# A hybrid decoder layer on one core: two branches' accumulators are copied out of PSUM by ScalarE, and VectorE multiplies the copies in a queue of lower priority

## The chip, the cores and the metric

The kernel runs on one core of a Trainium2 chip. The core has five engines that run side by side, each through a fixed list of instructions of its own: TensorE (PE in the rows; its weight loads stand apart as PEld), VectorE (DVE), ScalarE (ACT), GpSimd (POOL) and SyncE (SP), which issues the transfers here. An engine stops at an instruction whose operands are not ready, and everything behind it in its list waits too. Weights and activations lie in SBUF; PE writes its sums into PSUM, a small memory of banks. The metric is the device time of one execution, in microseconds (us).

## The reference, cut to what matters

One decoder layer is applied to 1024 prompt tokens and 32 sample tokens (8 sequences of 4), with a width of 1024. From a normalised input `h` four branches are computed: A a diagonal state space model (SSM), B a gated convolution, C a gated delta rule, D stick-breaking attention. Each gives 256 values a token. They are projected to the full width, each is multiplied by a sigmoid gate, and the four are added:

```
branches = jnp.stack([y_a, y_b, y_c, y_d], axis=2)
br    = jnp.einsum('blnw,nwd->blnd', branches, p['w_branch'])
gates = jax.nn.sigmoid(h @ p['w_gate']).reshape(bsz, L, N_BRANCH, D_MODEL)
mixed = jnp.sum(gates * br, axis=2) @ p['w_o']
x = layer_norm(ALPHA_DN * x + (1.0 + g1) * mixed, p['ln1_g'], p['ln1_b'])
```

Behind it come the feed-forward part and a second norm. The change is in the product `gates * br` of two of the four branches.

## The kernel before, in words

**Tiling.** The 1056 tokens are three blocks of 352 (`TB`), the width is eight slabs of 128 channels (`m`). A value is kept as the sum of two half-precision parts, so a product takes three matmuls (`mm3`, line 87 in the rows). One gate tile, 128 channels by 352 tokens, is a sum of 24 matmuls `gps<-h,whl` into one PSUM bank. The projection of the branch to the same channels is six matmuls `gps<-y,wbr` into a second bank, `pb`. Both come from one pool of three banks, `gps`; the conditioning product (`ada_slab`, matmuls `gps<-chl,whl`) takes its banks there too.

**The gate step** (`gates`, lines 1472 to 1495). ScalarE takes the tanh of the gate sum into an SBUF tile `gth` (line 1490; the sigmoid is half of one plus a tanh). VectorE forms `(gth + 1) * pb` with one scalar_tensor_tensor (STT for short), which reads `pb` in PSUM (line 1494, or line 1492 for the first branch). GpSimd adds the product to the running sum `mix` (`merge`, line 1523). `gates(1)` with `first=True` serves branch B and is not touched. `gates(3)` for D and `gates(2)` for C, eight slabs of three blocks each, are the 48 tiles in question. The gates of A (`gates7`, lines 1755 to 1773) use other code: an STT with a PSUM operand at line 1770 and an addition of two SBUF tiles at line 1519, both of the same 128x352 size.

**Weights.** `load_w` brings a slab of 512 KB into one of three tiles `wraw` (transfers `wraw<-in_w_gate`, `wraw<-in_w_ada`); ScalarE scales it (line 105) and makes the upper half-precision part (line 108), GpSimd the remainder (line 114, `whl<-wraw,whl`). Only then is a `wraw` tile free for the next transfer.

**Order.** The Tile framework fixes each engine's list when the kernel is built. Each instruction carries a priority from the stream in which it was written, a lower number goes first among those that its planner holds to be ready: `hot` -8 million, `sup` -4 million, the ordinary text and `br` from 0, `br2` 2 million, `lo` 4 million, `bg` 8 million. Gate matmuls are `lo`: they fill PE between the chains of branches C and A. The tanh, the STT and the merge are `sup`.

**Stages.** The 48 tiles run beside two chains. First the delta rule (lines 890 to 1145). Then the SSM (`ssm`): parameters and tables of cosine and sine (`cs`, `sn`, `tw`, complex multiplications at line 1220, on VectorE and GpSimd), projected matrices (`car`, `cai`, `ab`, `bd`, transposed by PE to `sps`), a small recurrence that goes through DRAM (`kd`, `tt`, line 1358), the scan (`gg`, `hr`, `hi`), the output `yo`, then GELU and GLU (`gs`, `gx`, `yh`, lines 1440 to 1468). Last come the sums for `gates7` (`r`, `tf`, lines 1710 to 1719 and 116).

Of the kernel before, what the change touches and what calls it, by code (L numbers as in the profile page):

```python
# [9 lines left out]
F32 = mybir.dt.float32  # L10
F16 = mybir.dt.float16
I32 = mybir.dt.int32
AF = mybir.ActivationFunctionType
ALU = mybir.AluOpType
# [3 lines left out]
P = 128  # L18
# [7 lines left out]
TB = 352  # L26
# [47 lines left out]
class Builder:  # L74
# [1397 lines left out]
    def gates(self, n, y, first, last, ms=range(KD), ada=0):  # L1472

        nc, I = self.nc, self.I
        pg = self.pg
        for m in ms:
            for _ in range(ada):
                self.ada_slab(self.ada_next)
                self.ada_next += 1
            if m % 4 == 0:  # L1480
                self.branch_w(n * 2 + m // 4)
            w = self.load_w(I["w_gate"][n * KD + m])
            for b in range(NTB):
                ps = self.gtile()
                xh, xl = self.hx(b * TB, TB)
                self.gemm(ps[:, :TB], w, KD, xh, xl)
                pb = self.branch(y, m, b)
                with self.sup:
                    th = pg.tile([P, TB], F32, name="gth", tag="gth", bufs=3)
                    nc.scalar.activation(th, ps[:, :TB], AF.Tanh, scale=IS / 2)  # L1490
                    if first:
                        nc.vector.scalar_tensor_tensor(self.mix[b][:, m], th, 1.0, pb, op0=ALU.add, op1=ALU.mult)
                    else:
                        nc.vector.scalar_tensor_tensor(th, th, 1.0, pb, op0=ALU.add, op1=ALU.mult)  # L1494
                        self.merge(m, b, th, last)

    def branch_w(self, i):
        nc = self.nc
# [496 lines left out]
def build(ctx, tc, I, O, stop=None):  # L1995
    B = Builder(ctx, tc, I, O)
    B.wraw_bufs, B.whl_bufs = 3, 4
    B.consts()
    B.wp = B.pool("w")
    B.gp = B.gp2 = B.pool("gps", bufs=3, space=PSUM)  # L2000
    hp = B.pool("hp")
    yp = B.pool("yp", bufs=2)
    B.make_h(hp)
    B.prep_consts()
    if stop:
        B.attention(yp)
        if stop == "B":
            B.conv_branch(yp)
        if stop == "C":
            B.delta(yp)  # L2010
            B.delta_sample()
            B.delta_rec(yp)
        if stop == "A":
            B.ssm_u()
            B.ssm(yp)
        return B
    def between():
        B.conv_branch(yp)
        B.ssm_u()
        B.px = B.pool("mx", side="right")  # L2020
        B.mix = [B.px.tile([P, KD, TB], F32, name="mix%d" % b, tag="mx", bufs=NTB) for b in range(NTB)]
        B.pg = B.pool("gate", side="right")
        B.gates(1, B.yB, True, False, range(0, GSPLIT))

    B.attention(yp, between)
    B.delta(yp, lambda i: B.gates(1, B.yB, True, False, range(GSPLIT + i, GSPLIT + i + 1)))
    with B.br2:
        B.delta_sample()
    B.delta_rec(yp)
    B.gates(3, B.yD, False, False, ada=A3)  # L2030
    B.gates(2, B.yC, False, False, range(2 * G7), ada=A2)
    B.ssm(yp)
    g7 = B.pool("gate7", side="right")
    B.np = None
    B.up_t = g7
    B.gp = B.pool("gps7", bufs=5, space=PSUM)
    Tf = g7.tile([P, 4, 2, 4, NTB, HB], F16, name="tf")
    for b in range(NTB):
        for q in (0, 2):
            B.sums7(B.h, Tf, b, g7.tile([P, 8 * HB], F32, name="r7", tag="r7"), slice(q, q + 2))  # L2040
    B.xh7 = B.forms7(B.h, Tf)
    B.sk = B.pool("gate7w", side="right")
    B.ska = B.sk
    B.gates7(2, B.yC, False, range(G7, KD // 2))
    B.gates7(0, B.yA, True, range(KD // 2))
    B.free(B.gp, B.gp2, yp, hp, B.ska, g7, B.pg)
    B.np = B.pool("nps2", space=PSUM)
    B.gp = B.pool("gps2", bufs=6, space=PSUM)
    B.px1 = B.pool("x1", side="right")
    B.ph2 = B.pool("h2", side="right")  # L2050
    B.afp = B.pool("af")
    B.mixer_out()
    B.ffn()
    B.close()
    return B
# [125 lines left out]
```

## Time and profile before

| | |
|---|---|
| median of 3 runs | 1922.05 us (1920.45 to 1927.18) |
| the profiled execution | 1922.55 us, its span 1920.8 us |
| granted TensorE clock, mean of the span | 0.96 |
| busy: PE, DVE, ACT, POOL | 90%, 67%, 51%, 50% |

Times in rows are us from the start of the span. An engine's busy share is an average over the span; how its work is spread is seen by stretches. An entry in square brackets behind an instruction is the time for which its engine sat idle before it, with the instruction that ended the wait.

### The profile page before, as it was taken

The numbers are of one execution on the slowest core, as the hardware profiler recorded it, in microseconds if no ns is written. First come the engines' busy times: TensorE is split into PE (matmuls) and PEld (weight loads), VectorE is DVE, ScalarE is ACT, GpSimd is POOL, SyncE is SP. The second block draws the span as 40 slices with busy tenths as digits, with TensorE's granted clock in tenths as the row PEclk, the third lists the DMA queues.
The fourth block names the chain that finished last, engine by engine and source line by source line (L and its number), as shares of the span: only waits on it lengthen the run. The fifth ranks groups of instructions, "written<-read, shape, count | busy, mean of one in ns | idle before, by whom it ended". The sixth has DMA issues, their size and how long they took to land.

```text
span 1920.8 us, 36538 instructions
## 1 busy us (share of the span) xinstructions
PE 1736.0 (90%) x14985; PEld 1202.0 (63%) x14985; DVE 1289.1 (67%) x2134; ACT 988.2 (51%) x1836; POOL 963.0 (50%) x952
## 2 busy tenths in 40 slices
PE   7899999999899998788689899988998999989996
PEld 3466666666666665555367555556776677767765
DVE  6763677659576756377986479777556656765648
ACT  4643454465655545235564655645575545554434
POOL 1827311222354545744550643278676667766633
PEclk9999999999999999899799999998999999999999
DMA  8222221121311112312331430001111112111112
GB/s 311 76 91 69 67 59 34 39 68 55 90 52 57 56 52 87 73 42 79 107 114 66 145 121 1 1 23 51 49 62 50 47 43 67 56 37 53 50 28 91
DMA packets 63616, 130.60 MB, mean 68 GB/s; under 512 B 16408, under 2 KB 35928, under 8 KB 63192
## 3 DMA queue, kind: packets, MB, share of 16 engines
q1 hardware_dynamic: 61912, 124.07, 20.9%
q0 software_dynamic: 1536, 4.20, 0.7%
q8 instruction: 117, 1.92, 0.4%
q14 instruction: 51, 0.42, 0.1%
HBM read 117.36 MB, written 10.88 MB: 67 GB/s over the span
## 4 chain that ended last, share of the span: by engine, by line
PE 40%; DVE 27%; ACT 10%; POOL 8%; DMA 8%; issue 5%; SPq 1%; ACTq 0%; DVEq 0%; POOLq 0%
PE gps L87 29%; DMA wraw<-in_w_up 2%; DVE ring L116 2%; PE x L87 2%; DVE af L1862 2%; POOL whl L1631 2%; DMA wraw<-in_w_down 1%; PE nps L87 1%; DVE dacc L758 1%; DVE af L1850 1%; PE dp L87 1%; DMA wraw<-in_w_gate 1%; PE z L87 1%; PE pada L87 1%; PE sps L87 1%
## 5 line engine op out<-in xcount | busy, mean ns | idle before, releaser
L87 PEld LDWEIGHTS <-whl 128*128 128x128 f16 x6992 | 629.1, 100 | 383.8 <-issue 91.1
L87 PE MATMUL gps<-h,whl 128*128 128x352 f16 (+1 forms) x4344 | 694.7, 315 | 48.0 <-ACT ct L1682 14.9
L87 PEld LDWEIGHTS <-wf 128*128 128x128 f16 x2232 | 198.9, 100 | 70.4 <-issue 12.0
L1631 POOL TENSOR_TENSOR whl<-wraw,whl 128x512 f16<-128x512 f32 (+1 forms) x136 | 166.3, 1234 | 95.2 <-ACT whl L1630 93.3
L114 POOL TENSOR_TENSOR whl<-wraw,whl 128x1024 f16<-128x1024 f32 (+1 forms) x66 | 150.5, 2281 | 85.4 <-ACT whl L108 83.6
L1679 DVE TENSOR_TENSOR ct<-ct,gps 128x352 f32<-128x352 f32 (+1 forms) x114 | 50.9, 449 | 189.8 <-ACT ct L1682 100.8
L1631 POOL TENSOR_TENSOR wf<-wraw,wf 128x512 f16<-128x512 f32 (+1 forms) x102 | 128.2, 1267 | 97.5 <-ACT wf L1630 95.6
L105 ACT ACTIVATE wraw<-wraw 128x1024 f32<-128x1024 f32 (+2 forms) x96 | 96.4, 1005 | 135.1 <-DMA wraw<-in_w_gate 45.7
L87 PE MATMUL gps<-tf,whl 128*128 128x176 f16 (+1 forms) x1152 | 145.9, 285 | 20.9 <-ACT ct L1682 16.3
L87 PE MATMUL gps<-ring,whl 128*128 128x352 f16 (+1 forms) x864 | 103.8, 276 | 8.1 <-ACT ct L1682 5.2
L87 PE MATMUL gps<-y,wbr 128*128 128x352 f16 x576 | 103.2, 313 | 6.7 <-DVE gth L1494 2.3
L1682 ACT ACTIVATE ct<-gps 128x352 f32<-128x352 f32 (+1 forms) x174 | 65.7, 393 | 77.4 <-PE gps L87 50.5
L1622 ACT ACTIVATE wraw<-wraw 128x1024 f32<-128x1024 f32 (+1 forms) x68 | 66.4, 976 | 75.2 <-DMA wraw<-in_w_down 37.8
L1523 POOL TENSOR_TENSOR mix<-mix,gth 128x352 f32<-128x352 f32 x48 | 53.0, 1104 | 99.1 <-DVE gth L1494 88.3
L87 PE MATMUL gps<-mix,wo 128*128 128x352 f16 x576 | 89.7, 316 | 5.3 <-DVE mix L118 2.4
L116 DVE TENSOR_TENSOR ring<-af,ring 128x352 f16<-128x352 f32 (+2 forms) x134 | 87.5, 684 | 5.6 <-ACT ring L108 5.6
L1630 ACT ACTIVATE whl<-wraw 128x512 f16<-128x512 f32 (+1 forms) x136 | 76.7, 585 | 26.8 <-POOL wraw L1635 13.5
L108 ACT ACTIVATE whl<-wraw 128x1024 f16<-128x1024 f32 (+1 forms) x82 | 84.9, 1035 | 3.6 <-DMA wraw<-in_w_ada 3.1
L87 PE MATMUL gps<-h,wf 128*128 128x352 f16 (+1 forms) x624 | 78.5, 281 | 7.8 <-DVE gth L1494 6.2
L108 ACT ACTIVATE ring<-af 128x352 f16<-128x352 f32 (+2 forms) x134 | 54.5, 430 | 56.0 <-DVE af L1862 46.5
L87 PEld LDWEIGHTS <-wo 128*128 128x128 f16 x576 | 56.4, 99 | 39.1 <-issue 4.2
L87 PEld LDWEIGHTS <-wbr 128*128 128x128 f16 x576 | 55.5, 98 | 36.5 <-issue 7.1
(622 smaller groups left out, 3364.9 us busy)
## 6 DMA issues: line engine op xcount, KB each, us to landing
wraw<-in_w_up SPq DMA_DIRECT2D x44, 512.0 KB, 3.5
wraw<-in_w_gate SPq DMA_DIRECT2D x32, 512.0 KB, 3.5
wraw<-in_w_ada SPq DMA_DIRECT2D x32, 512.0 KB, 3.6
wraw<-in_w_in SPq DMA_DIRECT2D x20, 512.0 KB, 3.7
wraw<-in_w_down SPq DMA_DIRECT2D x24, 384.0 KB, 3.1
x<-in_xT SPq DMA_DIRECT2D x12, 704.0 KB, 8.5
araw<-in_w_ada SPq DMA_DIRECT2D x16, 512.0 KB, 10.2
wraw<-in_w_branch SPq DMA_DIRECT2D x8, 512.0 KB, 3.6
```

What stands on the lines that cost most here:

```text
L87: self.nc.tensor.matmul(out, lhsT=lhsT, rhs=rhs, start=start, stop=stop, skip_group_check=resume)
L105: nc.scalar.activation(src, src, AF.Copy, scale=scale)
L108: nc.scalar.activation(hi, src, AF.Copy, scale=scale)
L114: nc.gpsimd.tensor_tensor(lo, src, hi, op=ALU.subtract)
L116: nc.vector.tensor_tensor(lo, src, hi, op=ALU.subtract)
L1523: nc.gpsimd.tensor_tensor(o, o, g, op=ALU.add)
L1622: nc.scalar.activation(raw, raw, AF.Copy, scale=SW)
L1630: nc.scalar.activation(hi, src, AF.Copy)
L1631: nc.gpsimd.tensor_tensor(lo, src, hi, op=ALU.subtract)
L1679: add = lambda o, p: nc.vector.tensor_tensor(o, o, p, op=ALU.add)
L1682: nc.scalar.activation({0: c11, 2: c12, 3: c22}[f], ps, AF.Copy)
L1862: sub = lambda o, p, q: nc.vector.tensor_tensor(o, p, q, op=ALU.subtract)
```

## The change

For the 48 tiles, ScalarE now does two things: the tanh of the gate sum, as before, and a plain copy of the branch sum `pb` from PSUM into a new SBUF tile `pbc` (four buffers, a pool `gate_b` of its own). VectorE multiplies in place, `(gth + 1) * pbc`, from two SBUF tiles, and this STT and the merge behind it are written in `br2` (2 million) instead of `sup` (-4 million). The number of instructions on PE, DVE, POOL and SP stays; ACT has 48 more.

```
                     if first:
                         nc.vector.scalar_tensor_tensor(self.mix[b][:, m], th, 1.0, pb, op0=ALU.add, op1=ALU.mult)
                     else:
-                        nc.vector.scalar_tensor_tensor(th, th, 1.0, pb, op0=ALU.add, op1=ALU.mult)
-                        self.merge(m, b, th, last)
+
+                        pc = self.pb.tile([P, TB], F32, name="pbc", tag="pbc", bufs=4)
+                        nc.scalar.activation(pc, pb, AF.Copy)
+                if not first:
+                    with self.br2:
+                        nc.vector.scalar_tensor_tensor(pc, th, 1.0, pc, op0=ALU.add, op1=ALU.mult)
+                        self.merge(m, b, pc, last)
...
     B.delta(yp, lambda i: B.gates(1, B.yB, True, False, range(GSPLIT + i, GSPLIT + i + 1)))
+    B.pb = B.pool("gate_b", side="right")
...
-    B.free(B.gp, B.gp2, yp, hp, B.ska, g7, B.pg)
+    B.free(B.gp, B.gp2, yp, hp, B.ska, g7, B.pb, B.pg)
```

In the changed kernel the lines behind the edit stand five or six lines further down: the copy is L1496, the STT L1499, the merge L1528.

Since the framework works the order out anew, other instructions move too. Three places follow.

ScalarE, in the SSM's first part, the list before: tanh (L1490) and scaling (L105) alternate.

```order
L294 ACTIVATE adat<-gps,c_b_ada 128x9
L108 ACTIVATE whl<-wraw 128x1024
L1490 ACTIVATE gth<-gps 128x352
L105 ACTIVATE wraw<-wraw 128x1024
L1490 ACTIVATE gth<-gps 128x352
L105 ACTIVATE wraw<-wraw 128x1024
L1338 ACTIVATE bq<-sps 128x512 x4
```

The same place in the changed kernel:

```order
L294 ACTIVATE adat<-gps,c_b_ada 128x9
L108 ACTIVATE whl<-wraw 128x1024
L1490 ACTIVATE gth<-gps 128x352
L1496 ACTIVATE pbc<-gps 128x352
L105 ACTIVATE wraw<-wraw 128x1024 x2
L1490 ACTIVATE gth<-gps 128x352
L1496 ACTIVATE pbc<-gps 128x352
L1490 ACTIVATE gth<-gps 128x352
L108 ACTIVATE whl<-wraw 128x1024
L1496 ACTIVATE pbc<-gps 128x352
L1338 ACTIVATE bq<-sps 128x512 x4
```

The second tanh now stands behind two scalings instead of one, and three copies stand ahead of `bq`, which belongs to the SSM.

GpSimd, in the same stretch, before: two weight remainders (L114) stand in the chain of cosine and sine tables.

```order
L1220 TENSOR_TENSOR cs<-cs,tw 128x8x8
L1220 TENSOR_TENSOR tw<-sn,cs 128x8x8
L1220 TENSOR_TENSOR cs<-cs 128x8x16
L1220 TENSOR_TENSOR sn<-sn,tw 128x8x8
L1523 TENSOR_TENSOR mix_1940<-mix_1940,gth 128x352
L1220 TENSOR_TENSOR tw<-sn 128x8x16
L1220 TENSOR_TENSOR sn<-cs,sn 128x8x16
L1220 TENSOR_TENSOR cs<-cs,tw 128x8x16
L114 TENSOR_TENSOR whl<-wraw,whl 128x1024
L1220 TENSOR_TENSOR tw<-sn,cs 128x8x16
L1220 TENSOR_TENSOR cs<-cs 128x8x32
L114 TENSOR_TENSOR whl<-wraw,whl 128x1024
```

The same place in the changed kernel:

```order
L1220 TENSOR_TENSOR cs<-cs,tw 128x8x8
L114 TENSOR_TENSOR whl<-wraw,whl 128x1024
L1220 TENSOR_TENSOR tw<-sn,cs 128x8x8
L1220 TENSOR_TENSOR cs<-cs 128x8x16
L114 TENSOR_TENSOR whl<-wraw,whl 128x1024
L1528 TENSOR_TENSOR mix_1941<-mix_1941,pbc 128x352
L1220 TENSOR_TENSOR sn<-sn,tw 128x8x8
L1528 TENSOR_TENSOR mix_1939<-mix_1939,pbc 128x352
L1220 TENSOR_TENSOR tw<-sn 128x8x16
```

Both remainders move forward in the list: seven instructions of the list before that stood ahead of the first now stand behind it, among them six pieces of the tables.

VectorE, at the end of the same stretch, before:

```order
L1220 TENSOR_TENSOR big<-piv,bd 128x8x128
L1220 TENSOR_TENSOR ab<-prv,bd 128x1024
L1494 SCALAR_TENSOR_TENSOR gth<-gth,gps 128x352
L1220 TENSOR_TENSOR ab<-ab,big 128x1024
L1220 TENSOR_TENSOR big<-piv,bd 128x8x128
L1494 SCALAR_TENSOR_TENSOR gth<-gth,gps 128x352
L1220 TENSOR_TENSOR ab<-ab,big 128x1024
```

The same place in the changed kernel:

```order
L1220 TENSOR_TENSOR big<-piv,bd 128x8x128
L1220 TENSOR_TENSOR ab<-prv,bd 128x1024
L1220 TENSOR_TENSOR ab<-ab,big 128x1024
L1499 SCALAR_TENSOR_TENSOR pbc<-gth,pbc 128x352
L1220 TENSOR_TENSOR big<-piv,bd 128x8x128
L1220 TENSOR_TENSOR ab<-ab,big 128x1024
```

One STT still stands ahead of the last `ab`, now with the last `big` behind it as well.

## Rows read from the trace of the kernel before

**Rows 1.** The page: busy time of each engine, and the chain that ended last.
```profile
PE 1736.0 (90%) x14985; PEld 1202.0 (63%) x14985; DVE 1289.1 (67%) x2134; ACT 988.2 (51%) x1836; POOL 963.0 (50%) x952
...
PE 40%; DVE 27%; ACT 10%; POOL 8%; DMA 8%; issue 5%; SPq 1%; ACTq 0%; DVEq 0%; POOLq 0%
```

**Rows 2.** Busy us by stretch: PE, PEld, DVE, ACT, POOL; then PE's granted clock.
```profile
546.00:735.00 189.00, 178.64 (x2324) 119.50 (x2323) 121.33 (x260) 99.51 (x182) 95.48 (x82) 0.98 0.17 55
735.00:876.00 141.00, 113.61 (x798) 76.03 (x798) 80.23 (x181) 49.27 (x113) 76.50 (x76) 0.89 0.29 75
876.00:985.00 109.00, 80.03 (x624) 52.45 (x623) 103.57 (x122) 67.50 (x111) 58.98 (x42) 0.84 0.30 99
```

**Rows 3.** Busy us in the scan, columns as in rows 2.
```profile
818.00:855.00 37.00, 28.01 (x219) 18.36 (x219) 35.33 (x46) 13.60 (x30) 20.64 (x11) 0.95 0.15 48
```

**Rows 4.** Line 1494, the multiplication: durations (ns) and what it waited for.
```profile
L1494 DVE SCALAR_TENSOR_TENSOR gth<-gth,gps x48: 494/513/522, 549.8 to 941.7; 128x352 f32<-128x352 f32 x48
...
  PE gps L87: 29.0, 8
```

**Rows 5.** PE's waits, us 540 to 990: total us, times, longest.
```profile
PE gps L87 <- DVE gth L1494: 16.0, 6, 6.2
PE gps L87 <- ACT gth L1490: 9.6, 4, 5.2
```

**Rows 6.** Line 1490, the tanh of PSUM into SBUF (ns: least, median, most).
```profile
L1490 ACT ACTIVATE gth<-gps x72: 436/463/473, 273.3 to 935.2; 128x352 f32<-128x352 f32 x72
```

**Rows 7.** Timeline, us 785 to 822: the next transfer's scaling, and the start of the scan.
```profile
785.53 1.06 ACT L105 ACTIVATE wraw<-wraw 128x1024 f32<-128x1024 f32 x1 [1.73 <-DMA wraw<-in_w_ada]
...
813.59 5.74 PE L87 MATMUL gps<-h,whl 128*128 128x352 f16 x23 [4.55 <-DVE gth L1494]
...
821.33 1.22 DVE L1220 TENSOR_TENSOR gg<-cs,sr 128x1024 f32<-128x1024 f32 x1 [1.54 <-ACT sr L1382]
...
821.62 1.06 PE L87 MATMUL gps<-y,wbr 128*128 128x352 f16 x6
```

**Rows 8.** Timeline, us 769 to 787: how a multiplication comes to hold the SSM.
```profile
769.81 0.31 POOL L1220 TENSOR_TENSOR tw<-sn,cs 128x64 f32<-128x64 f32 x1
...
776.67 2.12 POOL L114 TENSOR_TENSOR whl<-wraw,whl 128x1024 f16<-128x1024 f32 x1
...
778.81 0.33 SPq L142 DMA_DIRECT2D wraw<-in_w_gate  x1
...
779.70 2.11 POOL L114 TENSOR_TENSOR whl<-wraw,whl 128x1024 f16<-128x1024 f32 x1
...
782.40 1.06 ACT L105 ACTIVATE wraw<-wraw 128x1024 f32<-128x1024 f32 x1 [12.95 <-DMA wraw<-in_w_gate]
...
783.89 0.52 DVE L1494 SCALAR_TENSOR_TENSOR gth<-gth,gps 128x352 f32<-128x352 f32 x1 [7.86 <-ACT gth L1490]
...
784.33 2.00 DVE L1220 TENSOR_TENSOR ab<-ab,big 128x1024 f32<-128x1024 f32 x1
...
786.39 0.90 PE L100 MATMUL sps<-ident,ab 128*128 128x128 f32 x3 [7.61 <-DVE ab L1220]
```

**Rows 9.** Line 1519 by itself (ns: least, median, most), and the stretch of its 24.
```profile
L1519 DVE TENSOR_TENSOR gth<-gth,mix x24: 508/518/2452, 977.9 to 1067.0; 128x352 f32<-128x352 f32 x24
...
977.00:1068.00 91.00, 85.02 (x807) 63.11 (x806) 62.58 (x113) 51.20 (x104) 22.36 (x15) 1.00 0.21 68
```

**Rows 10.** VectorE groups, us 970 to 1070: busy us, mean ns, idle before.
```profile
L1519 DVE TENSOR_TENSOR gth<-gth,mix 128x352 f32<-128x352 f32 x24 | 18.9, 803 | 0.1
...
L1770 DVE SCALAR_TENSOR_TENSOR gth<-ct,gps 128x352 f32<-128x352 f32 x24 | 11.8, 513 | 6.9 <-ACT ct L1757 6.9
```

**Rows 11.** Timeline near us 829: a multiplication beside a weight remainder on POOL.
```profile
828.84 2.12 POOL L114 TENSOR_TENSOR whl<-wraw,whl 128x1024 f16<-128x1024 f32 x1
828.88 0.51 DVE L1494 SCALAR_TENSOR_TENSOR gth<-gth,gps 128x352 f32<-128x352 f32 x1
...
829.32 2.73 DVE L1220 TENSOR_TENSOR gg<-gg,hr 128x1024 f32<-128x1024 f32 x1
```

## The prediction

> **What bounds the kernel now.** The page first: PE is busy for 90% of the span, the others for 50 to 67%, and the chain that ended last lies on PE for 40% and on VectorE for 27% [rows 1]. These are averages over stages with different limits, so the stretches in which the 48 tiles run come next [rows 2]. From 546 to 735 us (the delta rule) PE is busy for 178.6 of 189 us at a granted clock of 0.98: PE is the limit. From 735 to 876 (the SSM) no engine is full (PE 113.6, DVE 80.2, POOL 76.5 of 141): a chain of waits is the limit. From 876 to 985 DVE is busy for 103.6 of 109 us while PE idles and has a clock of 0.84: VectorE is the limit. What the change does to PE's banks can therefore pay in the first two stretches, what it does to VectorE costs in the last and in that part of the second, 818 to 855, where DVE is busy for 35.3 of 37 us [rows 3].
>
> Then the line itself. The 48 multiplications took 494 to 522 ns each and waited 29.0 us for PE [rows 4]. PE in turn waited 16.0 us in six pieces for a bank that they emptied, and 9.6 us in four for one that the tanh emptied [rows 5]. These 25.6 us look like the prize, but a wait of a filler is worth something only where nothing else holds the stage.
>
> **The change part by part.**
>
> *The copies.* 48 copies of 128x352 from PSUM into SBUF. The tanh has this shape, operands and engine, and takes 463 ns [rows 6]: 48 x 0.463 = 22.2 us on ScalarE. It is busy for 99.5 of 189, 49.3 of 141 and 67.5 of 109 us in the three stretches [rows 2], so idle time covers them: 0. Without that cover a copy costs its 0.46 us, and up to 1.06 us more while it waits for its six matmuls [rows 7] with the SSM's ScalarE work queued behind it.
>
> *The delta stage.* PE is nearly full; the most that freed banks can give is its whole idle time, 189 - 178.6 = 10.4 us, most of which belongs to the delta chain. I take 0, with a tenth to a half of that either way.
>
> *The end of the first SSM part.* Here one STT held the chain: it sat 7.86 us behind a tanh, which stood on ScalarE behind the scaling of a gate weight; that weight's transfer went out at 778.81, when GpSimd had ended the remainder of 776.67; behind the STT waited `ab`, behind `ab` PE for 7.61 us [rows 8]. In the new order the first remainder stands where `tw<-sn,cs` stood at 769.81, the second two small table pieces later. Step by step, for the second: 769.81 + 2.12 (first remainder) + about 1.7 (two pieces) + 2.11 = 775.7, and its tile is free. Its transfer takes 3.6 us, as the first one's 778.81 to 782.40: 779.4. Scaling 1.06, tanh 0.46, copy 0.46, STT 0.51: 781.9. Then `big`, of the size of `ab`, at most 2.0: `ab` starts at 783.9 instead of 784.33. So moving the remainders forward pays for the second scaling that now stands ahead of the tanh: -0.4. Bounds: -7.9, if the STT no longer holds anything; +5.7, if the second scaling stays at 785.53 [rows 7], since 785.53 + 1.06 + 0.46 + 0.46 + 0.51 + 2.0 = 790.0. I take -0.4, because the order shows the remainders moved and no new wait ahead of them. The table pieces that the remainders pass end about when they did: the same work, in another order.
>
> *The start of the scan.* PE sat 4.55 us until an STT emptied a bank, and `gg`, the first piece of the scan, started 1.54 us after VectorE was ready [rows 7]. With the copy in the STT's place the bank is free early and PE reaches the matmuls for `sr` sooner: -1.5, bounds -1.5 and +1.0 (two copies and their matmuls in front of the last `sr`). What is late next is the transfer of `tt`, which does not move by this.
>
> *The multiplication from SBUF.* The count is the same. Alone, an operation of this size on two SBUF tiles takes as long as one with a PSUM operand: line 1519 at least 508 ns, median 518 [rows 9], line 1770 513 in the mean [rows 10]. Beside GpSimd it does not: 24 of line 1519 took 803 ns in the mean and up to 2452, while the 24 of line 1770, in the same stretch and with an operand in PSUM, stayed at 513 [rows 9, 10]. Near 829 us the two kinds stand side by side: the STT with PSUM took its 0.51 us beside a GpSimd remainder, `gg` behind it 2.73 against 1.22 elsewhere [rows 7, 11]. So the edit brings the STT into this kind: 0.803 - 0.513 = 0.29 us each, in a stretch where GpSimd was busy for 22.4 of 91 us. It counts where VectorE is the limit: four STTs from 818 to 855 and seven from 876 to 985, 11 x 0.29 = 3.2 us. Bounds: 0 (each beside an idle GpSimd) and 11 x (2.452 - 0.513) = 21.3 us. I take 3.2, the nearest row; scaled to GpSimd's share in those stretches (20.6 of 37 and 59.0 of 109, rows 2 and 3) it would be 4 x 0.65 + 7 x 0.63 = 7.0.
>
> The Trainium skill, "SBUF — State Buffer", section "Who interferes with whom", gives a cause: a VectorE instruction with two SBUF inputs and a GpSimd instruction that reads SBUF share one read interface, and the one that starts second stands still until the other is done. The rows of line 1519 against line 1770 agree. By that rule an STT that meets a remainder of 2.1 us waits half of it on average, 1.05 us; at a GpSimd share of 0.55 this is 0.58 us each, 6.4 us for eleven, an estimate, against the 3.2 taken above.
>
> "VectorE: DVE Perf Modes", section "Rules for kernel authors", in the Trainium skill advises to copy PSUM to SBUF first only where many operations follow. Here one follows, and the rows agree that it becomes no faster by itself (508 against 513): by this page the copy is worth what the bank is worth, no more.
>
> *The lower priority.* In the list of VectorE the STTs move by a few places only; by the end of the last stretch all are done. Nothing waits for a merge before `gates7`. 0; bounds -1 and +1, two STTs of 0.5.
>
> *Sum.* -0.4 - 1.5 + 3.2 = +1.3. The profiled execution took 1922.55 (span 1920.8 and 1.75 around it), so 1923.85; that execution was 0.5 above the median of the three runs, so 1923.35, rounded to **1923**. A measurement of this kernel tells about 0.3%, 5.8 us, from no change: this is no change.
>
> **The rivals.**
>
> *Banks matter more (faster).* If the new order ends the hold-up at 783.89 altogether, `ab` starts when its own inputs are there: -7.9, and -1.5 at the scan, with few conflicts with GpSimd: 1922.5 - 9.4 = 1913. For it: PE's 25.6 us of bank waits, four times what the forecast needs, and copies that empty a bank in 0.46 us. Against it: the STT still stands ahead of `ab`, its tanh still behind a transfer, and the longest of the waits for a bank, 6.2 and 5.2 us [rows 5], are no longer than what VectorE's full stretch hides. If half of PE's idle time in the delta stage goes as well, 1908.
>
> *The shared memory interface (slower).* The place: the eleven STTs in the two stretches in which VectorE is full. The price: 7.0 us by GpSimd's share, and since a remainder or merge can be held up by an STT just as well, up to as much again on the table chain and the weights. With the small gains not arriving, 1922.5 + 7.0 = 1930, the worst 1943. It decides from some 8 us on, that is 0.7 us a piece. For it: 803 against 513 ns. Against it: the STTs in question often ran while GpSimd was idle, for the merges follow them.
>
> *ScalarE's list (slower).* The tanh that holds `ab` now waits for two scalings and two copies; if the remainders do not come as early as their place in the list says, `ab` starts at 790.0: +5.7, and with the 3.2 for the conflicts 1931. Against it: GpSimd has hardly a gap there, so place is time.
>
> *It doesn't do what it says:* the lower priority reorders nothing that is waited for and the copy frees a bank that was not missed. Then only the conflicts are left, 1925.5, inside the forecast's own range.
>
> **How the numbers follow.** Forecast with the last case 0.36; banks 0.33; the interface 0.18; ScalarE's list 0.13. That gives faster by over 0.3% (below 1916.3) 0.33, within 0.36, slower (above 1927.8) 0.31. The likeliest case has 1917 to 1928 for its own. The range leaves out a tenth at each side: 1907 (the banks case with part of the delta stage) and 1938 (the interface case at two thirds of its worst).
>
> **What would show it.** The copies: 48 of about 0.46 us on ScalarE. The conflicts: the line of the STT with a maximum far above 0.52 us and a mean near 0.8; if it stays at 0.51, the term of 3.2 is wrong. The first SSM part: `ab` at about 784, the tanh ahead of it behind two scalings. The scan: no idle time of VectorE ahead of `gg`, no wait of PE for a bank before it. PE's waits for line 1494's successor should be near zero, those for ScalarE larger; if they vanish and the stage ends no earlier, banks were not its limit. The prediction is wrong if the delta stage, for which it has 0, becomes longer or shorter by more than 3 us, or if the part behind 985 us does.

## The result: slower by 0.6%, and not where the forecast had the cost

The changed kernel took 1935.94 us in the median of 5 runs (1929.53 to 1937.32), the kernel before, beside it, 1922.42. The ratio is 1.0059, 95% interval 1.0042 to 1.0076: slower by 0.6%, clear of no change. A second set of 7 runs of the same kernel gave 1934.62 (1926.49 to 1940.93), ratio 1.0057 (1.0037 to 1.0077). The runs of the changed kernel spread over 14 us; 24 of the kernel before, beside that second set, had a median of 1921.51 (1919.00 to 1930.65). The profile below is of an execution of 1929.53 us, span 1927.7; a later one of 1940.63 us, span 1938.9, shows the rest.

The page and the three stretches, changed kernel, to be read against [rows 1, 2]; the columns are the same.

```profile
PE 1737.3 (90%) x14985; PEld 1202.0 (62%) x14985; DVE 1291.7 (67%) x2134; ACT 1004.1 (52%) x1884; POOL 968.8 (50%) x952
...
PE 37%; DVE 28%; ACT 10%; POOL 10%; DMA 8%; issue 6%; SPq 1%; ACTq 0%; DVEq 0%; POOLq 0%
```

```profile
546.00:735.00 189.00, 179.02 (x2301) 118.48 (x2300) 121.99 (x258) 104.45 (x203) 91.04 (x79) 0.96 0.17 53
735.00:876.00 141.00, 112.68 (x792) 74.75 (x790) 82.52 (x182) 55.55 (x126) 85.06 (x76) 0.89 0.29 72
876.00:985.00 109.00, 77.88 (x588) 50.32 (x588) 94.45 (x110) 66.33 (x113) 55.72 (x39) 0.80 0.31 103
```

The sums hardly differ. VectorE's last stretch seems emptier (94.5 against 103.6 us), because the work arrives there later: over the whole span VectorE is as busy as before (1291.7 against 1289.1 us). So the shares do not tell where 7 us went; landmarks do. The table gives when the same instruction starts in the two traces, and in the trace of the later execution.

| instruction | before | changed, 1929.5 us | changed, 1940.6 us |
|---|---|---|---|
| delta rule, `kd<-dp,cols`, sixth | 648.2 | +2.5 | +7.3 |
| delta rule, `S<-u`, fifteenth | 710.5 | +8.1 | +10.2 |
| transfer `par`, start of the SSM | 735.6 | +5.8 | +7.7 |
| last `ab` | 784.3 | +8.5 | +10.0 |
| transfer `kd`, first | 796.1 | +10.3 | +9.8 |
| `gg`, start of the scan | 821.3 | +11.3 | +11.1 |
| transfer `sy`, first half of the output | 863.0 | +6.9 | +8.4 |
| transfer `sy`, second half | 871.8 | +6.9 | +15.3 |
| transfer of the first `w_o` | 1004.3 | +6.8 | +16.0 |
| end of the span | 1920.8 | +6.9 | +18.1 |

In the first execution the loss arises in the delta stage (5.8 us at its end), grows through the first part of the SSM and is partly given back before the output. The second execution was 4.8 us late already at the first `kd<-dp,cols`, so only 2.9 of its 7.7 us arise in the delta stage; its loss nearly doubles within the output itself. Behind 1004 us it changes by 0.1 and 2.1 us.

**The delta stage**, from the first `kd<-dp,cols` to `par`: before, then the changed kernel in the first and in the second execution.

```profile
545.32:735.60 190.28, 179.32 (x2329) 119.96 (x2327) 122.45 (x265) 99.75 (x183) 96.20 (x82) 0.98 0.17 56
```

```profile
545.49:741.36 195.87, 184.90 (x2339) 122.15 (x2337) 125.16 (x268) 109.31 (x211) 96.87 (x82) 0.97 0.17 54
```

```profile
550.12:743.31 193.19, 181.86 (x2339) 121.40 (x2337) 125.08 (x268) 109.44 (x212) 96.78 (x82) 0.98 0.17 55
```

PE's idle time is the same in all three (11.0, 11.0 and 11.3 us). What has grown is PE's busy time, by 5.6 and 2.5 us. Ten more of the branches' matmuls fall into the stage (x2339 against x2329); six take 1.06 us [rows 7], so the ten are at most some 1.8 us of work that was done later before. Most of the rest of the 5.6 us is the granted clock. Before, it falls once, in the first execution of the changed kernel twice:

```profile
660.00:670.00 10.00, 6.39 (x137) 4.50 (x133) 6.25 (x11) 6.08 (x11) 4.00 (x6) 0.89 0.01 2
670.00:680.00 10.00, 10.00 (x93) 6.14 (x92) 7.16 (x19) 2.81 (x6) 5.48 (x6) 0.77 0.01 2
```

```profile
640.00:650.00 10.00, 10.00 (x127) 6.83 (x124) 3.76 (x12) 4.28 (x9) 1.55 (x2) 0.66 0.10 40
...
670.00:680.00 10.00, 7.88 (x51) 4.36 (x49) 9.10 (x17) 4.08 (x10) 6.68 (x8) 0.74 0.01 2
680.00:690.00 10.00, 10.00 (x117) 5.77 (x117) 5.36 (x12) 3.88 (x7) 4.11 (x3) 0.92 0.01 2
```

What the clock withheld is, as an estimate from these rows, (0.11 + 0.23) x 10 = 3.4 us before and (0.34 + 0.26 + 0.08) x 10 = 6.8 us here. The second execution had one such fall, as before.

**The lines of the changed operations.** First the multiplication (line 1499), then the copy (1496), answering to [rows 4, 6].

```profile
L1499 DVE SCALAR_TENSOR_TENSOR pbc<-gth,pbc x48: 499/519/2280, 551.7 to 950.7; 128x352 f32<-128x352 f32 x48
...
  ACT pbc L1496: 46.5, 10
```

```profile
L1496 ACT ACTIVATE pbc<-gps x48: 437/457/721, 550.2 to 944.8; 128x352 f32<-128x352 f32 x48
...
  PE gps L87: 7.9, 11
```

```profile
L1499 DVE SCALAR_TENSOR_TENSOR pbc<-gth,pbc 128x352 f32<-128x352 f32 x48 | 33.2, 694 | 46.8 <-ACT pbc L1496 46.5
```

Single multiplications now take up to 2.28 us, and the mean has gone from 513 to 694 ns, as forecast in kind. The copy takes its 0.46 us and waits 7.9 us in all for its matmuls. PE's waits for a bank, against [rows 5]:

```profile
PE gps L87 <- ACT gth L1490: 24.8, 7, 11.3
PE gps L87 <- DVE whl L118: 10.2, 3, 5.9
...
PE gps L87 <- ACT pbc L1496: 3.6, 1, 3.6
```

The 16.0 us for the multiplication have shrunk to 3.6 us for the copy; the 9.6 for the tanh have grown to 24.8. The wait for one bank was exchanged for the wait for another. (The row in the middle is a wait for a part of a weight, not for a bank.)

**The first SSM part**, changed kernel, answering to [rows 8]:

```profile
778.02 3.10 POOL L114 TENSOR_TENSOR whl<-wraw,whl 128x1024 f16<-128x1024 f32 x1
...
782.69 2.12 POOL L114 TENSOR_TENSOR whl<-wraw,whl 128x1024 f16<-128x1024 f32 x1
...
784.66 1.06 ACT L105 ACTIVATE wraw<-wraw 128x1024 f32<-128x1024 f32 x1 [15.01 <-DMA wraw<-in_w_gate]
...
788.53 1.06 ACT L105 ACTIVATE wraw<-wraw 128x1024 f32<-128x1024 f32 x1 [2.81 <-POOL tw L1220]
...
789.99 0.45 PE L87 MATMUL gps<-y,wbr 128*128 128x352 f16 x1 [11.34 <-ACT gth L1490]
...
790.40 0.72 DVE L1499 SCALAR_TENSOR_TENSOR pbc<-gth,pbc 128x352 f32<-128x352 f32 x1 [8.20 <-ACT pbc L1496]
791.04 1.70 DVE L1220 TENSOR_TENSOR big<-piv,bd 128x1024 f32<-128x1024 f32 x1
...
792.78 1.83 DVE L1220 TENSOR_TENSOR ab<-ab,big 128x1024 f32<-128x1024 f32 x1
```

The remainders did move forward against what stands round them, the tanh still waits behind two scalings, the multiplication still holds VectorE (8.20 against 7.86 us), and `big` follows it. Measured from `par`, `ab` starts 2.7 us later than before (8.5 - 5.8). PE stands for 11.3 us, its longest wait, with a gate's bank full and the tanh behind the second scaling.

**The start of the scan**, changed kernel, answering to [rows 7]. Between the fifth and the sixth of the eight `sr`, ScalarE's list now has a tanh, a copy and two weight parts (line 108); before, the sixth followed 0.7 us behind the `si` of the fifth.

```profile
828.64 0.57 ACT L1490 ACTIVATE gth<-gps 128x352 f32<-128x352 f32 x1
828.99 1.16 ACT L108 ACTIVATE whl<-wraw 128x1024 f16<-128x1024 f32 x1
829.93 0.57 ACT L1496 ACTIVATE pbc<-gps 128x352 f32<-128x352 f32 x1
830.28 1.16 ACT L108 ACTIVATE wbr<-wraw 128x1024 f16<-128x1024 f32 x1
831.23 0.40 ACT L1382 ACTIVATE sr<-sps 128x145 f32<-128x145 f32 x1
```

The sixth starts 2.4 us behind the `si` of the fifth (828.86 to 831.23), and the eighth ends at 832.36. VectorE is then about to end a multiplication that took 2.20 us (830.54) beside a remainder on GpSimd, and `gg` starts at 832.66; so that slow multiplication costs at most 0.3 us here. VectorE's work on `tt`, from which the `sr` follow, ends 9.5 us later than before (826.88 against 817.37), `gg` starts 11.3 us later; the 1.8 us between the two match the longer stop in ScalarE's list.

**The output of the SSM.** ScalarE in the kernel before copies the first finished tiles (`yo`) at once; in the changed kernel both scalings of the GLU weights stand ahead of them. Before:

```profile
855.08 0.28 ACT L1428 ACTIVATE yo<-sps 128x128 f32<-128x128 f32 x1 [3.96 <-PE sps L87]
...
857.21 0.42 ACT L105 ACTIVATE wraw<-wraw 128x256 f32<-128x256 f32 x1 [1.07 <-DMA wraw<-in_w_glu]
```

Changed, ScalarE and then PE:

```profile
862.30 0.42 ACT L105 ACTIVATE wraw<-wraw 128x256 f32<-128x256 f32 x1 [5.45 <-DMA wraw<-in_w_glu]
862.62 0.45 ACT L1496 ACTIVATE pbc<-gps 128x352 f32<-128x352 f32 x1
865.44 0.42 ACT L105 ACTIVATE wraw<-wraw 128x256 f32<-128x256 f32 x1 [2.37 <-POOL mix L1528]
865.77 0.26 ACT L1428 ACTIVATE yo<-sps 128x128 f32<-128x128 f32 x1
```

```profile
866.14 0.50 PE L87 MATMUL sps<-U,tt 128*128 128x137 f32 x2 [1.50 <-ACT yo L1429]
867.24 0.50 PE L87 MATMUL sps<-U,tt 128*128 128x137 f32 x2
```

Here PE waits 1.50 us and then works at full clock, a group every 1.1 us. In the execution of 1940.6 us the same instructions, after the same wait:

```profile
865.85 0.50 PE L87 MATMUL sps<-U,tt 128*128 128x137 f32 x2 [1.49 <-ACT yo L1429]
866.98 0.83 PE L87 MATMUL sps<-U,tt 128*128 128x137 f32 x2
868.94 0.82 PE L87 MATMUL sps<-U,tt 128*128 128x137 f32 x2
```

A group takes 1.96 us. PE's busy time and clock in stretches of 4 us (the clock is the third figure from the end) show why:

```profile
864.00:868.00 4.00, 2.51 (x12) 1.60 (x11) 0.00 (x0) 2.28 (x14) 1.11 (x2) 0.86 0.14 33
868.00:872.00 4.00, 4.00 (x13) 2.98 (x14) 0.00 (x0) 0.69 (x4) 0.00 (x0) 0.50 0.00 0
...
884.00:888.00 4.00, 4.00 (x15) 2.56 (x14) 0.00 (x0) 1.01 (x5) 0.00 (x0) 0.50 0.20 42
888.00:892.00 4.00, 4.00 (x19) 2.29 (x18) 1.19 (x2) 1.25 (x2) 2.54 (x3) 0.66 0.87 237
```

The granted clock fell to half, the 1.2 GHz level, about a microsecond after that wait ended, and stayed there for 20 us of float32 output matmuls, with PE busy all the time; it rose again once the half-precision gate matmuls were back. This costs 6.9 us between the two halves of the output (15.3 - 8.4); all eleven groups take 20.7 us (865.85 to 886.58) instead of 12.0 (866.14 to 878.16). The kernel before has a fall here too, 0.63 between 856 and 860, but there PE runs fifteen half-precision gate matmuls before the output, and from 860 on, with the output, the clock is 1.00.

### The profile page after: what moved, and what is told of

Same layout as the page of the kernel before. It is cut to its first block, busy times and chain, and to the rows that moved or that the text cites. A ratio compares the mean times of both kernels' runs of the same rounds, so it can differ in the third digit from the quotient of the medians.

```text
span 1927.7 us, 36563 instructions
## 1 busy us (share of the span) xinstructions
PE 1737.3 (90%) x14985; PEld 1202.0 (62%) x14985; DVE 1291.7 (67%) x2134; ACT 1004.1 (52%) x1884; POOL 968.8 (50%) x952
## 4 chain that ended last, share of the span: by engine, by line
PE 37%; DVE 28%; ACT 10%; POOL 10%; DMA 8%; issue 6%; SPq 1%; ACTq 0%; DVEq 0%; POOLq 0%
PE gps L87 27%; DMA wraw<-in_w_up 2%; DVE ring L116 2%; DVE af L1867 2%; PE x L87 2%; POOL whl L1636 2%; POOL whl L114 1%; DMA wraw<-in_w_down 1%; PE nps L87 1%; DVE af L1855 1%; DVE dacc L758 1%; PE sps L87 1%; DVE tf L116 1%; DVE af L1853 1%; PE pada L87 1%
## 5 line engine op out<-in xcount | busy, mean ns | idle before, releaser
L87 PE MATMUL gps<-h,whl 128*128 128x352 f16 (+1 forms) x4344 | 686.7, 312 | 44.4 <-ACT ct L1687 15.0
L114 POOL TENSOR_TENSOR whl<-wraw,whl 128x1024 f16<-128x1024 f32 (+1 forms) x66 | 151.8, 2301 | 87.4 <-ACT whl L108 75.5
L105 ACT ACTIVATE wraw<-wraw 128x1024 f32<-128x1024 f32 (+2 forms) x96 | 96.5, 1005 | 138.2 <-DMA wraw<-in_w_gate 43.4
L87 PE MATMUL gps<-y,wbr 128*128 128x352 f16 x576 | 108.0, 323 | 23.2 <-ACT gth L1490 21.0
L1528 POOL TENSOR_TENSOR mix<-mix,pbc 128x352 f32<-128x352 f32 x48 | 61.0, 1271 | 97.7 <-DVE pbc L1499 89.7
```

Of the source, the lines that this page charges most:

```text
L87: self.nc.tensor.matmul(out, lhsT=lhsT, rhs=rhs, start=start, stop=stop, skip_group_check=resume)
L105: nc.scalar.activation(src, src, AF.Copy, scale=scale)
L114: nc.gpsimd.tensor_tensor(lo, src, hi, op=ALU.subtract)
L1528: nc.gpsimd.tensor_tensor(o, o, g, op=ALU.add)
```

## The experiments

Every time is a median beside the kernel before on the same chip; ratios are to that kernel, with a 95% interval. The first four share one set of runs of it (1921.02), the next four another (1919.71), the last three a third (1921.51).

The question was which part of the change does it: the operand in SBUF (GpSimd holds up the multiplication), the lower queue, or ScalarE's copies. Four kernels take them apart.

**The copies with the high queue.**

```
-                    with self.br2:
+                    with self.sup:
                         nc.vector.scalar_tensor_tensor(pc, th, 1.0, pc, op0=ALU.add, op1=ALU.mult)
                         self.merge(m, b, pc, last)
```

> The changed kernel with one part undone: the multiplication and the merge stay in the queue of high priority, the copies by ScalarE stay. Theory 'interface' (the multiplication from two SBUF tiles is held up by GpSimd, delays the delta chain, PE idles and its clock falls): still slow, 1930 to 1938 us, mean of the multiplication 0.65 to 0.85 us with single ones near 2. Rival 'priority' (the lower queue makes multiplications and merges late): back to 1922, within 4 us.

1933.61 us, ratio 1.0052 (1.0033 to 1.0070), a mean of 726 ns for the multiplication and a single one of 2.28 us. The queue is not the cause. All that the theory of the interface named came true, but the copies are in this kernel as well.

**The lower queue without copies.**

```
-                    else:
+                if not first:
+                    with self.br2:
                         nc.vector.scalar_tensor_tensor(th, th, 1.0, pb, op0=ALU.add, op1=ALU.mult)
                         self.merge(m, b, th, last)
```

> The other part alone: no copies, the multiplication reads the accumulator in PSUM as before, but it and the merge are in the lower queue. Theory 'interface': 1922 within 4 us, every multiplication at 0.49 to 0.53 us. Rival 'priority': 1930 to 1938, with PE waiting longer for the banks that the late multiplications hold (more than the 16 us before).

1917.51 us, ratio 0.9985 (0.9972 to 0.9997): the lower queue by itself is a small gain. The time is half a microsecond under the band of the first theory, and the multiplications are as short as it said (501 to 522 ns).

**Copies that nobody reads.** The multiplication takes PSUM again, in the high queue.

```
                         pc = self.pb.tile([P, TB], F32, name="pbc", tag="pbc", bufs=4)
                         nc.scalar.activation(pc, pb, AF.Copy)
-                if not first:
-                    with self.br2:
-                        nc.vector.scalar_tensor_tensor(pc, th, 1.0, pc, op0=ALU.add, op1=ALU.mult)
-                        self.merge(m, b, pc, last)
+                        nc.vector.scalar_tensor_tensor(th, th, 1.0, pb, op0=ALU.add, op1=ALU.mult)
+                        self.merge(m, b, th, last)
```

> The kernel before, with the 48 copies by ScalarE added; nobody reads them, the multiplication still takes its operand from PSUM in the high queue. Theory 'interface': 1922 within 4 us. Rival 'ScalarE' (the copies hold up what stands behind them in ScalarE's list): 1930 to 1938, with ScalarE busy for some 22 us more as in the changed kernel.

1930.18 us, ratio 1.0044 (1.0031 to 1.0057). The theory of the interface fails here: every multiplication is short, and most of the loss is there. (ScalarE is busy for 1003.0 us against 988.2, 15 us more and not 22: a copy starts before the instruction ahead of it has ended, as at 862.62 above.)

```profile
L1497 DVE SCALAR_TENSOR_TENSOR gth<-gth,gps x48: 494/512/522, 553.8 to 952.6; 128x352 f32<-128x352 f32 x48
```

**The tanh left in its bank.** All of the change, but the multiplication has one operand in PSUM.

```
-                    th = pg.tile([P, TB], F32, name="gth", tag="gth", bufs=3)
+                    th = pg.tile([P, TB], F32, name="gth", tag="gth", bufs=3) if first else ps[:, :TB]
```

> The changed kernel, copies and lower queue as they are, but the tanh of the 48 tiles is written back into its own PSUM bank, so that the multiplication has one operand in PSUM and one in SBUF. The gate's bank is then held until the multiplication, the branch's bank is free after the copy. Theory 'interface': every multiplication at 0.49 to 0.53 us and the time 1920 to 1927. Rivals 'priority' and 'ScalarE': as slow as the changed kernel, 1930 to 1938, since copies, queue and nearly all of the order are the same.

1933.76 us, ratio 1.0066 (1.0053 to 1.0079), and no multiplication is held up:

```profile
L1499 DVE SCALAR_TENSOR_TENSOR pbc<-gps,pbc x48: 502/518/526, 552.1 to 943.2; 128x352 f32<-128x352 f32 x48
```

But this kernel also keeps the gate's bank longer, and in its profile `par` goes out 14.2 us late, against 5.8 in the changed kernel: it is slow at another place and does not settle what the interface costs. That the loss is there without the interface is shown by the copies that nobody reads. What the interface adds to it is not told apart: between the copies that nobody reads and the copies with the high queue lie 1.0044 and 1.0052, whose intervals overlap, and in the second of the two the branch's bank is also free earlier. The Trainium skill's rule of the shared read interface ("SBUF — State Buffer", "Who interferes with whom") holds for the durations: 2.28 us at most with two operands in SBUF, 0.526 with one. What it does to this kernel's time is too small to be told.

The cause sits with the copies. Next: is it their time on ScalarE, and which of the two branches?

**Copies of something that is ready.** The same number and size, but of the tanh's result instead of `pb`; nobody reads them.

```
-                        nc.scalar.activation(pc, pb, AF.Copy)
+                        nc.scalar.activation(pc, th, AF.Copy)
```

(against the kernel with copies that nobody reads)

> The kernel before with 48 copies by ScalarE that nobody reads, as long as those of the accumulators, but of the tanh's own result: they wait for no matmul and hold no bank. Theory 'ScalarE's time and order' (22 us more work and another order are enough): 1926 to 1934, like the copies of the accumulators that nobody reads. Rival 'waits of the copies for the branch's matmuls': 1921 within 4 us.

1918.80 us, ratio 0.9992 (0.9982 to 1.0002): no difference. The copies took 488 ns each, longer than those of `pb`:

```profile
L1496 ACT ACTIVATE pbc<-gth x48: 478/488/505, 551.2 to 940.6; 128x352 f32<-128x352 f32 x48
```

So 48 more operations on ScalarE, with which it is busy for 1009.5 instead of 988.2 us, cost nothing, as the prediction had it. What costs is that a copy reads the branch's accumulator. That brings three things, which this run does not separate: the copy waits for PE's six matmuls with ScalarE's list behind it, it holds the bank until it is done, and the planner makes another order round it. The theory that more work and another order are enough has fallen, as far as this one other order goes.

**Branch D alone, branch C alone.**

```
-                    else:
+                    elif n != 3:
+                        nc.vector.scalar_tensor_tensor(th, th, 1.0, pb, op0=ALU.add, op1=ALU.mult)
+                        self.merge(m, b, th, last)
+                    else:
...
-                if not first:
+                if not first and n == 3:
                     with self.br2:
```

(the other kernel has 2 for 3)

> The change for branch D alone (24 tiles, beside the delta rule); branch C as before. Theory 'ScalarE's list' (the copies and the order that they bring delay the chain that is running at the time): only the delta stage is hurt, +2 to +7 us, 1923 to 1928, and the SSM's output matmuls run at full clock as before. Rival 'interface': about +1, since the delta stage has most of VectorE's idle time.

> The change for branch C alone (24 tiles, from the last part of the delta rule to the last sums); branch D as before. Theory 'ScalarE's list': the SSM is hurt, both scalings of the GLU weights stand ahead of the output's first copies, PE waits before its output matmuls and their clock falls in part of the executions: 1926 to 1932. Rival 'interface': +3 to +7, with the loss in the stretches in which VectorE is full and no difference ahead of them.

D alone: 1927.73, ratio 1.0040 (1.0025 to 1.0054). C alone: 1929.16, ratio 1.0052 (1.0036 to 1.0067). Each by itself loses most of what both lose; the parts do not add. In the profile of D alone the fifteenth `S<-u` of the delta rule comes 5.5 us late, in that of C alone, where the delta stage has few copies, 1.6 us. That fits the list's theory for D, and its output matmuls ran at full clock, though its 8.0 us exceed the 2 to 7 that were named; its profiled execution, at 1923.24 us the shortest of its six, shows less than half of them. From the first `kd<-dp,cols` to `par` the stage takes 192.3 to 195.9 us in all profiles with D's copies (204.0 where the tanh stays in its bank) and 190.3 to 191.5 in those without.

For C the expected place is not borne out. In its profile, of the shortest of its six (1926.71 us), one of the two scalings stands ahead of the first `yo` and the other behind four of them, as before. PE reaches the output without a wait, at full clock:

```profile
860.12 0.40 PE L87 MATMUL sps<-U,tt 128*128 128x137 f32 x2
860.44 0.50 PE L87 MATMUL sps<-hr,car 64*128 64x137 f32 x2
```

The first half of the output goes out only 0.8 us late. Where C alone loses its 9.4 us is not shown.

**The GLU weights behind the output.** All of the change, and the GLU weights' transfers are tied to the seventh output tile, so that their scalings cannot stand ahead of it; to that end the two loads are also written earlier, right behind the output.

```
+            if dep is not None:
+                nc.vector.tensor_copy(raw[:, 0:1], dep)
             nc.sync.dma_start(raw[:, :n], src)
...
+        ws = [self.load_w(I["w_glu"][i], dep=yo[0][:, 6, 0:1]) for i in range(2)]
         self.free(pq, pa)
...
-            w = self.load_w(I["w_glu"][i])
+            w = ws[i]
```

> The changed kernel with one thing moved: the two transfers of the GLU weights wait until the seventh of the sixteen output tiles is copied (a copy of one column ties them), so that their scalings stand behind the output's copies on ScalarE. Theory 'ScalarE's list': the wait of PE before the output matmuls (1.5 us) goes, the matmuls run at full clock in every execution, and 3 us of delay go as well: 1924 to 1930 in the median, 6 to 10 under the changed kernel. Rival (the loss has no place of its own, the order is just worse): no difference, 1932 to 1937.

1925.65 us, ratio 1.0028 (1.0018 to 1.0039), and no run of 12 above 1928.2. The interval lies below the first of the changed kernel's two and just touches the second: about half of the loss of the changed kernel goes with this place. PE reaches the output without a wait:

```profile
860.38 0.28 ACT L1430 ACTIVATE yo<-sps 128x128 f32<-128x128 f32 x1 [4.62 <-PE sps L87]
```

```profile
863.00 0.40 PE L87 MATMUL sps<-U,tt 128*128 128x137 f32 x2
863.98 0.50 PE L87 MATMUL sps<-U,tt 128*128 128x137 f32 x2
```

**The changed kernel again**, unaltered.

> The changed kernel once more, unaltered, beside the others on one chip, for another execution's profile. Theory (whether the clock falls in the SSM's output matmuls is decided anew in each execution): times spread over 1925 to 1938, median near 1934; if the profiled execution is one above 1933, its output matmuls stand at half the clock, some 2 us a group against 1.1 in the profile at hand. Rival (the spread has nothing to do with that stretch): the output matmuls at full clock whatever the time.

1934.62 us; the profiled execution, 1940.63, is the one shown above with the output at half the clock. The expectation holds, but that two of the seven lie above 1938: the same code, with the same 1.5 us of waiting, ran its output once at full and once at half clock. The copies that nobody reads and the copies with the high queue, with waits of 1.46 and 1.44 us at this place, had it at 0.50 in their profiles too. But the wait alone does not decide it. The copies of something ready have both scalings ahead of `yo` as well, and PE waits longer:

```profile
863.64 0.50 PE L87 MATMUL sps<-U,tt 128*128 128x137 f32 x2 [1.73 <-ACT yo L1429]
```

Their output ran at full clock, and their twelve runs, 1915.33 to 1923.99, lost nothing. What else it takes was not found.

**Branch C alone, with the GLU weights tied.**

```
+        ws = [self.load_w(I["w_glu"][i], dep=yo[0][:, 6, 0:1]) for i in range(2)]
```

(added to C alone)

> The change for branch C alone, and the transfers of the GLU weights tied behind the seventh output tile. Theory (the loss is the delta stage's order and the output behind the GLU weights, and both are taken away here): 1918 to 1923, no difference from before. Rival (the rest of the copies costs as well, in the last stretch or by the shared interface): 1925 to 1930.

1923.36 us, ratio 1.0007 (0.9998 to 1.0017): no difference from before, just above the band that was named. With the copies of D gone and the GLU weights tied, the loss is gone, within 0.17%. So the tie takes away what C alone loses, though C's profile has no wait at the output; what it removes there stays open.

**A version that beats both.** The lower queue without copies, and the GLU weights tied.

```
-                    else:
+                if not first:
+                    with self.br2:
                         nc.vector.scalar_tensor_tensor(th, th, 1.0, pb, op0=ALU.add, op1=ALU.mult)
                         self.merge(m, b, th, last)
...
+        ws = [self.load_w(I["w_glu"][i], dep=yo[0][:, 6, 0:1]) for i in range(2)]
```

> No copies, the multiplication from PSUM and the merge in the lower queue, and the GLU weights tied behind the seventh output tile: a candidate for a version that beats both. Theory: the lower queue alone gave 0.9985; the tie removes a wait that the kernel before has only in part, so 1914 to 1919. Rival: the late GLU weights hold up the GLU, 1919 to 1925.

1916.79 us, ratio 0.9972 (0.9960 to 0.9984): faster than the kernel before by 0.28%, than the changed one by some 0.9%. The lower queue alone gave 0.9985, with an interval that overlaps this one, so what the tie adds here is not shown.

## Why the prediction was right or wrong

The time lies in the range, but the forecast of no change (0.36) failed; the kernel is slower, which had 0.31. That the range held is luck: its upper end, 1938, was taken from the shared interface, and of the two slower rivals this one, with the larger chance, is not what the loss needs. The other, ScalarE's list, is borne out at `ab`, at the scan and at the output, of which only `ab` was priced; where C alone loses is open.

- *The copies at 0.* For ScalarE's time this is right: 48 copies of a ready tile cost nothing. For copies that read the accumulator it is wrong: with nobody reading them they cost 0.44%. The sentence on what a copy costs when the cover is gone, with the SSM's work queued behind it, named the danger and gave it no place.
- *The delta stage at 0.* Wrong: 5.6 us in one profile and 2.9 in the other, against a bound of half of 10.4 either way and a sign of being wrong at 3. PE's idle time was taken as the limit of a gain; for a loss it limits nothing, and it did not change. PE's busy time grew: in both by ten matmuls of the branches that moved into the stage, in the first also by a second fall of the granted clock, some 3.4 us. The fall to 0.66 between 640 and 650 us came after ten microseconds in which PE was busy for 7.5 (9.1 before). The stage is longer where D's copies are and not where only C's are. Whether by the waits for PE's branch matmuls or by the order that the planner made round them was not told apart: in the changed kernel's first profile no copy waits there for more than 2.5 us.
- *`ab` at -0.4.* Mis-sized: +2.7 from `par` to `ab`. The sum had the second scaling at 779.4, 43.8 us behind `par`; it came 47.2 us behind it (788.53 - 741.36), 3.4 us later. The first remainder began at 36.7 us instead of 34.2, and took 3.10 us instead of 2.12 beside a VectorE operation of 3.13. (With the high queue both remainders took 2.12 us and the second scaling came 47.2 us behind `par` all the same, so the 3.10 is not the whole of it.) Behind the second scaling waited the tanh, the copy and the multiplication, and PE for the bank that the tanh emptied. The bound of +5.7 holds, and so does its mechanism.
- *The start of the scan at -1.5.* Wrong in sign: `gg` moves from +10.3 at the last `tt` transfer to +11.3. That is the bound of +1.0, and its mechanism in part: what stands in front of the last three `sr` is a tanh, one copy and two weight parts, which hold the sixth 1.7 us longer than before. VectorE has no idle time ahead of `gg`, as named, but PE does wait for a bank before it: 4.17 us at 825.13, for a tanh.
- *The interface at 3.2.* Its size is 0.694 - 0.513 = 0.18 us each, 2.0 for eleven, near the 0.29 and far from the ends. (Line 1494 starts five times between 818 and 855, the last at 854.63, not four: with twelve the term would have been 3.5.) That this is a cost of the time was not seen: with short multiplications the copies lose 0.44%, with long ones 0.52%, which is not told apart.
- *The lower queue at 0, within 1.* Without copies it is worth 0.15% (0.03 to 0.28), 2.9 us, to the good; with them no gain is seen (1.0057 and 1.0059 against 1.0052).
- *PE's bank waits.* "Should be near zero" for the multiplication's successor: 3.6. Those for ScalarE larger: 24.8. And "if they vanish and the stage ends no earlier, banks were not its limit" is what came, except that they were exchanged rather than removed.
- *Not in the prediction at all:* the output of the SSM. The order of the changed kernel shows two scalings of 128x256 ahead of the first `yo`, where before one of them stood behind four of these. I read that stretch for copies of `pb` and not for what the copies had pushed forward. About half of the loss goes with this place.

## What to carry to other kernels

A copy that empties an accumulator early frees a bank, but it puts a wait for TensorE into the list of an engine that others need; ask whose work stands behind it, not how busy that engine is. When a schedule is made anew, compare the whole list of every engine on the critical stages, weight preparation included: about half of the loss here goes with operations that the diff does not contain. And a short wait of TensorE before a long run of float32 matmuls is worth a trial run without it: here its price differed from one execution to the next, from the wait itself to 8.7 us more, while another kernel had such a wait and lost nothing.

## What the runs showed of the hardware

In 20 us of float32 matmuls, with PE recorded as busy throughout, the granted clock stayed at 0.50, and it rose only in the stretch in which the half-precision gate matmuls came back; entered at 1.00, the same matmuls stayed at 1.00. In two executions of the same code the same wait of 1.5 us ahead of them led to either; in another kernel a wait of 1.73 us left them at 1.00. Here this fall took 8.7 us, so it can be a good part of the 14 us over which the changed kernel's runs spread, though not all; those of the kernel before spread over 7.2 us in 29 runs, 8.7 in 23 and 11.7 in 24.

A multiplication of 128x352 with two operands in SBUF took 0.50 to 2.28 us beside GpSimd's work, with one operand in PSUM 0.49 to 0.53 us, in each kernel in which all 48 have it.
